# A layer's first residual, computed through DRAM: placed behind the HGRN group, or behind retention's rotation

## The chip, the cores and the metric

The kernel runs on one core of a Trainium2 chip. The metric is the device time of one execution in microseconds (us); lower is better. The kernel before was timed three times: 2478.46 us median, 2472.77 to 2479.16.

## The reference, cut to what matters

Two layers (DEPTH = 2) work on x, 1024 rows by 1024 columns, float32. The part that the change touches is the term `DEEPNORM_ALPHA * h` in the first residual of each layer:

```
h = layer_norm(x, ln_in_g, ln_in_b)
for l in range(DEPTH):
    proj = h @ w_in[l]                       # 13 slices of 256 columns
    y_a = rglru_mixer(a_x, a_g, ...)         # group A, linear scan
    y_b = retention_mixer(r_q, r_k, r_v, r_g, ...)   # group B, rotary on q and k
    y_c = stick_breaking_mixer(s_q, s_k, s_v)        # group C, attention
    y_d = hgrn2_mixer(d_q, d_f, d_v, d_g, ...)       # group D
    mix = jnp.concatenate([y_a, y_b, y_c, y_d], axis=-1) @ w_out[l]
    h = layer_norm(DEEPNORM_ALPHA * h + mix, ln1_g[l], ln1_b[l])
    ff = jnp.square(jax.nn.relu(h @ w_up[l])) @ w_down[l]
    h = layer_norm(DEEPNORM_ALPHA * h + ff, ln2_g[l], ln2_b[l])
```

## The kernel before, in words

Most products run as three float32r matmuls on a high and a low part (`mm3`), so each weight tile is loaded, split by ScalarE (`hi`, L217) and VectorE (`lo`, L218), and multiplied on TensorE.

The normalised rows z of the layer's input are written to a DRAM tile `spill` as they are made (L850 for layer 0, L1285 for layer 1). `residual_spilled` (L815) turns them into `ALPHA * (z * g + b)`: it loads g and b, broadcast, into one 8 KB tile `rgb` (two DMAs, L819), scales it (L820), and then, for each of 16 pieces of 128 by 512, loads a tile `rs` from `spill` (L825), multiplies (L812), adds (L813) and writes it to a second DRAM tile `resid` (L827). All its DMAs are issued from GpSimd's queue (POOL). The output projection reads `resid` much later (L939, SyncE's queue), into the tiles z to which it adds its products (L954).

A layer's trace order is: projection of D's v and g (`proj_d`), `mixer_d`, `residual_spilled`, `mixer_c`, projection of retention's q and k (`proj_b`), `rotary`, projection of its v, projection of A (`proj_a`), `mixer_a`, projection of its g, `mixer_b`, output projection. `mixer_d` works head pair by head pair (hp); for each it makes 6 levels of intra-chunk scores and then a chain of state updates (L492) that feed the matmuls of L501. `mixer_c` goes block by block: scores `ps` (L572, L573), two activations `ca`, `cs` (L577, L578), a scan on VectorE (L580), a transpose (L592) and the product with v (L600).

The order of the instructions on the engines isn't the trace order. The kernel is built with `schedule_with_timeline_sim=True`: a planner simulates the engines and lets each engine take, of what is ready, what comes first in trace order; `boost()` puts a block ahead (the units of D, C, A and B). The order that the planner writes down is then fixed: each engine executes its list in order and waits at the head of it.

Tiles are taken from pools with a fixed number of buffers, and an instruction that opens a tile waits for a free one. Two pools matter here. `m` has 13 buffers of 2 KB: `rs`, D's q, k, f and products, C's `ca` and `cs`, A's `bd`, `axc`, `ar`, `ai`, `aa`. `u` has 4 of 8 KB: D's output `yd`, `rgb`, C's values `cv`, C's output `yc`, the rotation's work tile `rot`, A's output `ya`, B's `yb`. The PSUM pool `po` has one bank, shared by D, C and B.

Of the kernel before, what the change touches and what calls it, by code (L numbers as in the profile page):

```python
# [44 lines left out]
def trunk_kernel(ctx, tc, x, ln_in_g, ln_in_b, w_in, conv_w, conv_b, rg_wa, rg_ba, rg_wx, rg_bx, rg_lambda,  # L45
# [26 lines left out]
    def t_z(shape, nm, dt=F32):  # L72
        return big.tile(shape, dt, tag="z", name=nm, bufs=NZ)

    def t_u(dt, shape, nm):
        return big.tile(shape, dt, tag="u", name=nm, bufs=4)

    def t_m(shape, nm):
        return mid.tile(shape, F32, tag="m", name=nm, bufs=NM)
# [542 lines left out]
    def proj_b(l, act, which, dst):  # L622

        for s in which:
            i = (s - R_Q) % 2
            w = load_cols(w_in[l], seg(s), "wb")
            for pr in range(4):
                ps = gemm_tm_pair(w, act, pr)
                d = dst[pr][:, i]
                if s == R_G:  # L630
                    A.activation(d, ps, AF.Sigmoid)
                    V.tensor_tensor(out=d, in0=ps, in1=d, op=ALU.mult)
                else:
                    A.activation(d, ps, AF.Copy)

    def rotary(qk):

        wk = t_u(F32, [P, 2, 2, 512], "rot")
        for pr in range(4):
            for which in range(2):  # L640
                ct = wk[:, which, 0].rearrange("p (y h d) -> p y h d", y=2, d=32)
                tb = wk[:, which, 1].rearrange("p (h two d) -> p h two d", two=2, d=32)
                nc.sync.dma_start(out=ct, in_=c_rot[pr, which])
                d = qk[pr][:, which].rearrange("p t (h two d) -> p (t h) two d", two=2, d=32)
                V.tensor_tensor(out=tb[:, :, 0, :], in0=d[:, :, 1, :], in1=ct[:, 1], op=ALU.mult)
                V.tensor_tensor(out=tb[:, :, 1, :], in0=d[:, :, 0, :], in1=ct[:, 1], op=ALU.mult)
                V.tensor_tensor(out=d, in0=d, in1=ct[:, 0].unsqueeze(2).to_broadcast([P, 8, 2, 32]), op=ALU.mult)
                V.tensor_tensor(out=d[:, :, 0, :], in0=d[:, :, 0, :], in1=tb[:, :, 0, :], op=ALU.subtract)
                V.tensor_tensor(out=d[:, :, 1, :], in0=d[:, :, 1, :], in1=tb[:, :, 1, :], op=ALU.add)
# [160 lines left out]
    def residual(z, gb, bb):  # L810

        V.tensor_tensor(out=z, in0=z, in1=gb, op=ALU.mult)  # L812
        V.tensor_tensor(out=z, in0=z, in1=bb, op=ALU.add)  # L813

    def residual_spilled(g, b):  # L815

        r = t_u(F32, [P, 2, DM], "rgb")
        for i, v in enumerate((g, b)):
            nc.gpsimd.dma_start(out=r[:, i], in_=v.rearrange("(o d) -> o d", o=1).to_broadcast([P, DM]))  # L819
        V.tensor_scalar(out=r, in0=r, scalar1=ALPHA, scalar2=None, op0=ALU.mult)  # L820
        for nt in range(NT):
            for j in range(2):
                c = slice(512 * j, 512 * j + 512)
                t = t_m([P, 512], "rs")
                nc.gpsimd.dma_start(out=t, in_=spill[nt][:, c])  # L825
                residual(t, r[:, 0, c], r[:, 1, c])
                nc.gpsimd.dma_start(out=resid[nt][:, c], in_=t)  # L827
# [28 lines left out]
    res_g, res_b = ln_in_g, ln_in_b  # L856
# [15 lines left out]
    for l in range(DEPTH):  # L872
# [2 lines left out]
            vt, gt = [], []  # L875
            weave(proj_d(l, act, vt, gt))
        ys[3] = mixer_d(l, act, vt, gt)
        residual_spilled(res_g, res_b)
        ys[2] = mixer_c(l, act)
        qk = [t_z([P, 2, 2, 256], f"bqk{i}") for i in range(4)]  # L880
        proj_b(l, act, (R_Q, R_K), qk)
        rotary(qk)
        vg = [t_z([P, 2, 2, 256], f"bvg{i}") for i in range(4)]
        proj_b(l, act, (R_V,), vg)
        xs, gs = proj_a(l, act)
# [428 lines left out]
        res_g, res_b = ln2_g[l], ln2_b[l]  # L1314
# [66 lines left out]
```

## Time and profile before

| what | value |
|---|---|
| timed runs | 2478.46 us median of 3 |
| profiled execution, its own time | 2481.85 us |
| span of its instructions | 2480.1 us |
| mean granted TensorE clock | 0.982 |
| busy: PE, weight load, VectorE, ScalarE, GpSimd | 96%, 80%, 71%, 45%, 4% |

The span is the time from the first instruction to the last; 1.75 us of the execution lie around it. Durations below come from this one execution. "Granted clock" 1.00 is 2.4 GHz, 0.50 is 1.2 GHz. The rows of layer 0 lie between 100 and 600 us; the same stages of layer 1 come some 1226 us later.

### The profile page before, as it was taken

How to read it: one execution, taken by the hardware profiler on the slowest of the kernel's cores; microseconds unless marked ns; L12 is line 12 of the kernel's file. 1: busy time of each engine (PE TensorE's matmuls, PEld its weight loads, DVE VectorE, ACT ScalarE, POOL GpSimd, SP SyncE). 2: the span in 40 equal slices, each digit the busy share in tenths (PEclk: the TensorE clock that was granted, in tenths of full speed). 3: DMA queues.
4: the chain of work that ended last, by engine and by line, in shares of the span. 5: the costliest groups of instructions: out<-in, count | busy, mean ns of one | idle time of the engine just before them, and what ended most of it. 6: DMA issues, size and time to landing. Idle time of an engine off the chain costs nothing.

```text
span 2480.1 us, 34844 instructions
## 1 busy us (share of the span) xinstructions
PE 2386.4 (96%) x13924; PEld 1980.3 (80%) x13924; DVE 1757.0 (71%) x3016; ACT 1112.4 (45%) x1723; POOL 98.3 (4%) x180
## 2 busy tenths in 40 slices
PE   7999999999899999999999989999998999999997
PEld 6887888877688888888798878888777888888886
DVE  6468773657877877778655788556669777887778
ACT  5433655525543444434462336473264544445342
POOL 0002000000100000000000020000001000000000
PEclk9998999999899999999999989999999999999999
DMA  5215111220742233322212141112217333233322
GB/s 193 57 39 172 47 37 34 86 85 17 256 152 94 77 136 106 132 93 94 94 65 64 57 158 35 29 60 77 68 45 278 132 107 105 92 110 127 111 85 85
DMA packets 126970, 241.30 MB, mean 97 GB/s; under 512 B 8924, under 2 KB 81240, under 8 KB 118616
## 3 DMA queue, kind: packets, MB, share of 16 engines
q1 hardware_dynamic: 106032, 135.55, 17.0%
q0 software_dynamic: 19648, 102.80, 11.5%
q8 instruction: 110, 1.80, 0.3%
q10 hardware_dynamic: 1128, 0.72, 0.1%
q14 instruction: 52, 0.43, 0.1%
HBM read 201.29 MB, written 37.75 MB: 96 GB/s over the span
## 4 chain that ended last, share of the span: by engine, by line
PE 64%; issue 18%; DVE 12%; ACT 3%; DMA 2%; POOL 1%; SPq 0%; DVEq 0%; POOLq 0%; ACTq 0%
PE pg L256 17%; PE pt L256 11%; PE pg L248 8%; PE pg L247 8%; PE pg L249 8%; PE ps L256 5%; DVE z L999 3%; PE po L256 2%; DVE wdl L218 2%; DVE wd L996 1%; DVE u L996 1%; PE po L600 1%; DMA rs<-spill 1%; PE pt L592 1%; PE pt L202 1%
## 5 line engine op out<-in xcount | busy, mean ns | idle before, releaser
L218 DVE TENSOR_TENSOR wul<-wu,wuh 128x1024 fp32r<-128x1024 f32 x106 | 129.6, 1223 | 129.6 <-ACT wuh L217 59.6
L217 ACT ACTIVATE wuh<-wu 128x1024 fp32r<-128x1024 f32 x106 | 112.1, 1059 | 225.6 <-DVE wu L996 138.8
L256 PE MATMUL pg<-wdh,sa 128*128 128x512 f32 x560 | 182.0, 394 | 11.2 <-ACT sa L1189 7.2
L218 DVE TENSOR_TENSOR wdl<-wd,wdh 128x1024 fp32r<-128x1024 f32 x120 | 146.4, 1220 | 44.4 <-PE pt L256 23.2
L217 ACT ACTIVATE wdh<-wd 128x1024 fp32r<-128x1024 f32 x120 | 126.7, 1056 | 106.2 <-PE pg L256 71.6
L256 PE MATMUL ps<-wdh,sa 128*128 128x512 f32 x448 | 148.1, 396 | 8.2 <-ACT sa L1189 7.0
L256 PE MATMUL pt<-wdh,sa 128*128 128x512 f32 x448 | 146.7, 392 | 0.0
L256 PE MATMUL pt<-s,wuh 128*128 128x512 f32 x448 | 137.9, 389 | 0.0
L256 PE MATMUL pg<-s,wuh 128*128 128x512 f32 x448 | 136.1, 389 | 0.0
L256 PEld LDWEIGHTS pg<-wdh,sa 128*128 128x128 f32 x560 | 104.9, 189 | 38.4 <-ACT sa L1189 12.4
L247 PE MATMUL pg<-wo,yh 128*128 128x512 f32 x256 | 104.5, 408 | 9.0 <-DVE z L954 5.2
L256 PE MATMUL pg<-mh,wuh 128*128 128x512 f32 x280 | 108.9, 389 | 0.0
L256 PE MATMUL pg<-ml,wuh 128*128 128x512 f32 x280 | 108.9, 389 | 0.0
L256 PE MATMUL pg<-mh,wul 128*128 128x512 f32 x280 | 108.8, 389 | 0.0
L996 DVE TENSOR_TENSOR sa<-u,sa 128x512 fp32r<-128x512 f32 x140 | 90.9, 686 | 24.7 <-ACT sa L1189 24.7
L256 PEld LDWEIGHTS ps<-wdh,sa 128*128 128x128 f32 x448 | 85.3, 191 | 27.7 <-ACT sa L1189 7.8
L256 PE MATMUL pg<-wdl,sa 128*128 128x512 f32 x280 | 107.4, 392 | 0.0
L248 PE MATMUL pg<-wo,yh 128*128 128x512 f32 x256 | 103.4, 404 | 0.0
L249 PE MATMUL pg<-wo,yl 128*128 128x512 f32 x256 | 101.6, 403 | 0.2 <-DVE yl L899 0.2
L256 PEld LDWEIGHTS pt<-wdh,sa 128*128 128x128 f32 x448 | 85.1, 190 | 17.9
L1189 ACT ACTIVATE sa<-u 128x512 fp32r<-128x512 f32 x140 | 80.1, 623 | 42.4 <-PE pt L256 20.2
L256 PEld LDWEIGHTS pg<-s,wuh 128*128 128x128 f32 x448 | 84.1, 188 | 17.4
(400 smaller groups left out, 6806.2 us busy)
## 6 DMA issues: line engine op xcount, KB each, us to landing
s<-sd POOLq DMA_DIRECT2D x64, 1024.0 KB, 7.4
wu<-in_w_up_dram SPq DMA_DIRECT2D x64, 512.0 KB, 3.7
wd<-in_w_down_dram SPq DMA_DIRECT2D x64, 512.0 KB, 3.6
sd<-sx POOLq DMA_DIRECT2D x32, 512.0 KB, 8.3
spill<-z SPq DMA_DIRECT2D x16, 512.0 KB, 4.4
wb<-in_w_in_dram SPq DMA_DIRECT2D x16, 512.0 KB, 6.5
rs<-spill POOLq DMA_DIRECT2D x32, 256.0 KB, 4.2
resid<-rs POOLq DMA_DIRECT2D x32, 256.0 KB, 3.7
```

What stands on the lines that cost most here:

```text
L202: T.transpose(pt[:, j, i * P:(i + 1) * P], zs[i][:, k * P:(k + 1) * P], ident)
L217: A.activation(hi, raw, AF.Copy)
L218: V.tensor_tensor(out=lo, in0=raw, in1=hi.bitcast(F32), op=ALU.subtract)
L247: T.matmul(ps, ah, bh, start=(i == 0), stop=False)
L248: T.matmul(ps, ah, bl, start=False, stop=False)
L249: T.matmul(ps, al, bh, start=False, stop=(i == n - 1))
L256: T.matmul(ps, a, b, start=(first and i == 0 and j == 0), stop=(i == n - 1 and j == 2), skip_group_check=not first)
L592: T.transpose(pt[:, j * P:(j + 1) * P], s[:, j * P:(j + 1) * P], ident)
L600: T.matmul(po[DH * par:DH * par + DH, (nb % 4) * P:(nb % 4 + 1) * P], vt[:, kb, e:e + DH], wts[par][:, j * P:(j + 1) * P], start=(diag and ...
L996: V.tensor_tensor(out=out, in0=x, in1=y, op=ALU.subtract)
L999: V.tensor_tensor(out=out, in0=x, in1=y, op=ALU.add)
L1189: A.activation(hi, src, AF.Copy)
```

## The change

One call moves down, past `mixer_c`, the projection of retention's q and k, and the rotation. Nothing else is edited; the instructions of `residual_spilled` are the same.

```
         ys[3] = mixer_d(l, act, vt, gt)
-        residual_spilled(res_g, res_b)
         ys[2] = mixer_c(l, act)
         qk = [t_z([P, 2, 2, 256], f"bqk{i}") for i in range(4)]
         proj_b(l, act, (R_Q, R_K), qk)
         rotary(qk)
+        residual_spilled(res_g, res_b)
         vg = [t_z([P, 2, 2, 256], f"bvg{i}") for i in range(4)]
```

With it, the tiles `rgb` and `rs` stand behind `cv`, `yc`, `rot` and all `ca` and `cs` in the order in which the pools are asked.

## Rows read from the trace of the kernel before

**Rows 1.** The page, busy us by engine, with share of the span and count.

```profile
PE 2386.4 (96%) x13924; PEld 1980.3 (80%) x13924; DVE 1757.0 (71%) x3016; ACT 1112.4 (45%) x1723; POOL 98.3 (4%) x180
```

**Rows 2.** Stretches: length; busy us (count) PE, PEld, DVE, ACT, POOL; clock; DMA share; GB/s.

```profile
180.00:224.20 44.20, 44.18 (x573) 37.26 (x571) 39.53 (x89) 14.63 (x30) 14.61 (x27) 1.00 0.58 187
224.20:227.80 3.60, 0.00 (x0) 0.00 (x0) 2.18 (x5) 0.28 (x1) 1.63 (x3) 1.00 0.75 236
227.80:241.40 13.60, 11.35 (x72) 8.74 (x73) 12.65 (x35) 3.93 (x10) 2.17 (x4) 0.50 0.29 108
241.40:364.00 122.60, 121.22 (x1013) 101.81 (x1012) 98.75 (x199) 77.47 (x166) 0.00 (x0) 1.00 0.15 44
364.00:404.00 40.00, 40.00 (x279) 35.21 (x277) 5.56 (x7) 11.83 (x16) 0.00 (x0) 1.00 0.11 31
1449.80:1453.20 3.40, 0.30 (x12) 0.16 (x6) 2.17 (x4) 0.28 (x1) 1.62 (x3) 0.99 0.67 239
1453.20:1466.80 13.60, 10.28 (x69) 7.91 (x70) 13.34 (x36) 3.93 (x10) 2.72 (x5) 0.50 0.35 125
```

**Rows 3.** Chain that ended last, 215 to 242 us: start, us, what.

```profile
220.94 4.52 DMA rs<-spill
...
230.19 3.68 DMA resid<-rs
```

**Rows 4.** Waits, 216 to 241 us: who <- for whom: total us, times, longest.

```profile
ACT ca L577 <- DMA resid<-rs: 6.3, 2, 4.0
...
PE po L501 <- DVE df L492: 4.2, 2, 3.7
...
DVE rs L812 <- DMA rs<-spill: 3.4, 3, 1.5
...
ACT cs L578 <- DMA resid<-rs: 2.6, 1, 2.6
```

**Rows 5.** Waits, 1440 to 1467 us (layer 1).

```profile
ACT ca L577 <- DMA resid<-rs: 4.7, 1, 4.7
```

**Rows 6.** Instructions on tiles rs: count, ns min/median/max, first and last start.

```profile
L825 POOL DMA_DIRECT2D rs<-spill x32: 536/541/555, 183.8 to 1453.3; - x32
L812 DVE TENSOR_TENSOR rs<-rs,rgb x32: 666/685/693, 196.2 to 1458.3; 128x512 f32<-128x512 f32 x32
L813 DVE TENSOR_TENSOR rs<-rs,rgb x32: 676/685/693, 199.9 to 1459.3; 128x512 f32<-128x512 f32 x32
L827 POOL DMA_DIRECT2D resid<-rs x32: 539/544/561, 201.0 to 1460.3; - x32
```

**Rows 7.** The same on tile rgb, and its DMAs from issue to landing.

```profile
L820 DVE TENSOR_SCALAR rgb<-rgb x2: 1226/1226/1227, 194.8 to 1420.3; 128x2048 f32<-128x2048 f32 x2
...
DMA to landing us min/median/max: 6.9/7.6/8.3
```

**Rows 8.** VectorE in order of time, layer 0: start, us, what [idle before <- releaser].

```profile
360.21 0.42 DVE L649 TENSOR_TENSOR bqk<-bqk,rot 128x256 f32<-128x256 f32 x1
...
362.02 0.48 DVE L737 MEMSET bd<- 128x512 f32 x1
...
387.37 1.23 DVE L218 TENSOR_TENSOR wal<-wa,wah 128x1024 fp32r<-128x1024 f32 x1 [23.06 <-ACT wah L217]
```

**Rows 9.** Line 850, the writing of spill in layer 0.

```profile
L850 SPq DMA_DIRECT2D spill<-z x8: 319/360/1042, 12.1 to 34.8; - x8
```

**Rows 10.** Line 600 between 170 and 400 us.

```profile
L600 PE MATMUL po<-ca,cv x288: 272/273/324, 263.8 to 374.1; 128*64 128x128 f32 x144
```

**Rows 11.** Line 939, the reading of resid, both layers.

```profile
L939 SPq DMA_DIRECT2D z<-resid x16: 319/320/339, 462.8 to 1740.6; - x16
```

**Rows 12.** Waits, 290 to 330 us.

```profile
ACT ca L577 <- PE po L600: 9.8, 3, 3.7
...
PE pt L592 <- DVE cs L583: 1.0, 2, 0.6
```

**Rows 13.** ScalarE in order of time, retention's first evacuation.

```profile
258.07 0.60 ACT L634 ACTIVATE bqk<-pg 128x512 f32<-128x512 f32 x1 [3.40 <-DVE dat L509]
```

More of the change, by code (lines that the diff above doesn't have):

```diff
@@ L877, in trunk_kernel @@
         ys[3] = mixer_d(l, act, vt, gt)
-        residual_spilled(res_g, res_b)
         ys[2] = mixer_c(l, act)
@@ L882, in trunk_kernel @@
         rotary(qk)
+        residual_spilled(res_g, res_b)
         vg = [t_z([P, 2, 2, 256], f"bvg{i}") for i in range(4)]
```

## The prediction

> **What bounds the kernel now.** I read the busy line first. TensorE is busy 96% of the span and nothing else is above 71% [rows 1], so time is won only where TensorE stands still, runs at the lower clock, or waits inside a stage. Then I looked for stretches in which it does. Near the end of group D, TensorE does nothing from 224.2 to 227.8, and right behind that its granted clock is 0.50 (1.2 GHz) for 13.6 us; before and after it is busy throughout at 1.00. Layer 1 has the same pair of stretches, 3.4 us with 0.30 busy and 13.6 us at 0.50 [rows 2].
>
> Third, the chain that ended last and the waits say what held it. The chain through these 20 us runs over a load of the residual (4.52 us) and a store of it (3.68 us) [rows 3]. By engine: ScalarE, executing in order, waits 6.3 + 2.6 us to open `ca` and `cs` until stores of `rs` give buffers of pool m back; VectorE waits 3.4 us for loads of `rs`, with D's state updates (L492) queued behind them; TensorE waits 4.2 us for those updates [rows 4]. In layer 1 the `ca` wait is 4.7 us [rows 5]. So the residual does harm in three ways where it stands: 16 tiles through pool m in the middle of the change from D to C, VectorE blocked on DMAs, and VectorE's time itself, in 44 us in which it is 89% busy (39.53 of 44.20) [rows 2].
>
> **The change, part by part.**
>
> *Removed from the old place.* VectorE: 16 x (0.685 + 0.685) + 1.23 = 23.1 us a layer [rows 6, 7]. POOL: 16 x (0.541 + 0.544) = 17.4 us of issue, plus two for `rgb` [rows 6]. What this gives back I take from TensorE alone. Layer 0, 224.2 to 241.4: 17.2 us long; the work done is 0 + 11.35 x 0.50 = 5.7 us of the full clock; lost 11.5 us. Layer 1, 1449.8 to 1466.8: 17.0 us; work 0.3 + 10.28 x 0.50 = 5.4; lost 11.6 us [rows 2]. Together 23.1 us. With the waits gone TensorE should run on at 1.00, and the work behind shifts forward whole, since TensorE is busy 121.22 of the next 122.60 us and 40.00 of the 40 after that [rows 2]. Late next in the old place is D's own chain of state updates, which stays: some of its steps will still come a little late. That part no row prices; it lies between nothing and the 4.2 us that TensorE waits for L492 now [rows 4], and I take 1.0 us a layer, near the low end, because the 3.4 us that VectorE stood blocked on loads were most of it.
>
> *The clock.* It fell after 3.6 us without a matmul and came back 13.6 us later [rows 2], so 6.8 us of each layer's 11.5 are the clock's. The terms hang together: if the idle time goes, so does the low clock.
>
> *Added in the new place, VectorE.* The same 23.1 us. From 364 to 404 VectorE is busy 5.56 of 40 us, with one idle piece of 23.06 us before L218 at 387.37 [rows 2, 8]; room 34.4 us. TensorE is then busy with retention's v and A's projection. What would the cover cost if it were gone: VectorE blocked on an `rs` load at 387 delays the second half of A's weights; the longest such wait now is 1.5 us [rows 4].
>
> *When it can start.* `rgb` needs one of 4 buffers of u. With `yd`, `cv`, `yc` and `rot` ahead of it, the first to come back is `rot` (last use at 360.6) or `cv` (last use 374.1 + 0.3) [rows 8, 10]. So `rgb` is asked at about 361, lands 7.6 us later [rows 7] and is scaled by 370. Pool m has room at that time: `bd`, the first tile behind C's, is opened at 362.02 [rows 8], so loads of `rs` can be issued from then on. 22 us of VectorE from 370 make 392 the earliest end. If it takes as long as now (196.2 to about 234 in layer 0) it ends at 408, 4 us past that stretch. I take about 400 and price it at nothing.
>
> *Queues passed.* On POOL there is nothing between the old and the new place: it is idle from 241 to 404 [rows 2], so its 34 issues stand in nobody's way. On SyncE the first reading of `resid` is at 462.8 [rows 11], some 55 us behind the end that I expect; it would become late only if the residual ran on beyond 460. DMA: the engines are 11% busy there against 58% in the old stretch [rows 2], and the weights of A come through more crowded queues; 0 to 1 us, taken as 0. `rot` no longer waits for `rgb` to be done, worth nothing while TensorE is busy. `ya` takes the other of the two u buffers, free at 374.4, while A's second weights are split only at 387.37 [rows 8]; nothing.
>
> *Sum.* 2481.85 - (23.1 - 2 x 1.0) = 2481.85 - 21.1 = 2460.7 us in the profiled execution's own time. That execution is 3.4 us above the median of the timed runs, so the median should be 2460.7 - 3.4 = 2457.3: **2457 us**, 0.9% less.
>
> [...] I have taken busy matmuls as a full TensorE. The weight loads between 241.4 and 364 are busy 101.81 of 122.60 us, 83% [rows 2]. [...]
>
> **The rivals.**
>
> *A, slower: the loads run ahead of their scale.* Loads of `rs` need only `spill` and a buffer of m. In the old place the first was issued at 183.8, while VectorE first used one at 196.2 [rows 6], so loads do sit and wait for `rgb`. If the planner gives them buffers as soon as D lets go (about 184 to 197) but `rgb` has none until 361, they hold a good part of m's 13 buffers through all of C. For it: the idle POOL takes what is free. Against it: the same loads could have been issued long before 183.8 from `spill`, whose last write is issued at 34.8 [rows 9], and `bd`, which depends on nothing, was opened only behind C's last tiles [rows 8], so the pool seems to serve earlier tiles first. Price: even with 13 buffers C waits three times in 40 us for one (9.8 us on ScalarE), and TensorE then loses 1.0 us, 0.33 a wait [rows 12]. One such wait for each of C's 24 segments makes 8 us a layer; with ScalarE's full 3.25 us each it would be 78. I take 8 and the old stall kept, since its buffers are still missing: 2478.5 + 16 = 2495. It decides from 23.1 / 48 = 0.48 us of TensorE a segment if the old stall goes.
>
> *B, no change: the stall is D's own.* Retention's q and k are first evacuated at 258.07, released by D's last step [rows 13]; TensorE's other work there may be used up whatever the residual does, and D's chain of L492 would leave it idle again, with the low clock behind it. Against: the chain and three of the four waits name the residual's DMAs [rows 3, 4]. The time would be 2478, also if the planner left the residual where it is.
>
> *C, half the gain: a new stall where it lands.* VectorE, blocked on an `rs` load late in its list, holds up A's units; a gap as long as the old one brings the low clock as in [rows 2]. At half the old price, 5.8 us a layer, the median is 2457.3 + 11.6 = 2469. Against: TensorE is busy to the end of that stretch, and nothing that it does there reads what VectorE makes of the residual [rows 2].
>
> **How the numbers follow.** Forecast 0.69, A 0.11, B 0.10, C 0.10. About 0.3% (7.4 us) is what a measurement of this kernel can tell from no change. The forecast and two thirds of C lie below 2471: faster 0.76. B and the rest of C: same 0.13. A: slower 0.11. Range: low end 2457 - 11 = 2446, if D's chain costs nothing (2 us) and another piece of low clock falls away with the new order; the high end takes in C and B, 2479; A is left out.
>
> **What would show it.** Right: TensorE busy and at 1.00 through the end of D in both layers; no wait of `ca` or `cs` for `resid`; L812 first at about 360 (370, less the 11 us by which all behind D comes earlier), last before 400; VectorE's 23 us idle piece filled; z read from `resid` without a wait. Wrong: L825 issued near 185 again (A or B); TensorE waiting for L492 with the clock at 0.50 behind it (B); a new piece at 0.50 between 360 and 440 (C).

## The result, and the profile after

The changed kernel takes **2443.4 us** (median of 4 runs, 2440.3 to 2445.6), against 2475.6 for the kernel before in the same session (median of 4; the forecast went by the first three, 2478.5): ratio 0.9866, 95% interval 0.9846 to 0.9886, so 32 us less. I had forecast 2457 with a range from 2446. The direction and the mechanism of the stall came out, the gain is half as large again, and the time lies below the range. One execution of e3_behind_c, a version below, took 4760.6 us against 2446.6 to 2454.9 for its others, and is left out of its median.

The busy line of the changed kernel, for [rows 1]: TensorE has lost 19 us of busy time on the same 13924 matmuls, so a good part of the gain is clock; VectorE has as much to do as before.

```profile
PE 2367.4 (97%) x13924; PEld 1967.0 (80%) x13924; DVE 1759.4 (72%) x3016; ACT 1115.6 (46%) x1725; POOL 99.4 (4%) x180
```

Three stretches of it, columns as in [rows 2]: the end of D in layer 0, the same in layer 1, and the residual's new place. The pieces with next to no matmul (3.6 and 3.4 us) and the 13.6 us at 0.50 behind each are gone; where the residual now runs, TensorE is busy throughout at 1.00.

```profile
200.00:233.20 33.20, 33.20 (x325) 26.90 (x323) 21.44 (x60) 14.69 (x33) 0.00 (x0) 1.00 0.11 33
1404.00:1438.00 34.00, 34.00 (x330) 27.67 (x330) 22.48 (x63) 14.76 (x32) 0.00 (x0) 1.00 0.11 33
353.20:393.20 40.00, 40.00 (x271) 35.14 (x270) 27.12 (x41) 11.33 (x15) 14.68 (x26) 1.00 0.67 236
```

The residual's instructions, for [rows 6, 7], with the last of layer 0 from VectorE's order of time. The loads are issued at 348.8, behind the two of `rgb`, and the work ends at 384.0, ahead of the 400 that I had allowed.

```profile
L825 POOL DMA_DIRECT2D rs<-spill x32: 536/541/1133, 348.8 to 1572.7; - x32
L812 DVE TENSOR_TENSOR rs<-rs,rgb x32: 621/683/692, 355.0 to 1587.1; 128x512 f32<-128x512 f32 x32
```

```profile
383.35 0.68 DVE L813 TENSOR_TENSOR rs<-rs,rgb 128x512 f32<-128x512 f32 x1
```

**Where the time came from.** I cut each layer at three events: the first matmul of D's intra-chunk scores (L413, their diagonal), A's first activation (L729), and the first row normalised behind the output projection (L962). Windows of the kernel before, then of the changed one, layer 0 and then layer 1. Each pair of stretches holds the same matmuls (2584, then 884), so their lengths can be compared.

```profile
105.55:393.36 287.81, 280.57 (x2584) 236.00 (x2583) 205.50 (x446) 122.80 (x252) 18.41 (x34) 0.98 0.22 67
393.36:564.08 170.72, 162.47 (x884) 134.55 (x883) 98.16 (x260) 76.51 (x99) 0.00 (x0) 0.94 0.22 70
1331.46:1618.45 286.99, 279.86 (x2584) 235.53 (x2583) 205.55 (x446) 122.76 (x253) 18.44 (x34) 0.98 0.21 67
1618.45:1783.05 164.60, 156.82 (x884) 129.94 (x883) 97.63 (x259) 76.42 (x99) 0.00 (x0) 0.98 0.23 72
```

```profile
103.86:380.21 276.35, 275.13 (x2584) 232.24 (x2583) 205.84 (x444) 122.90 (x253) 18.12 (x33) 1.00 0.21 67
380.21:542.36 162.15, 156.64 (x884) 130.60 (x883) 99.09 (x262) 77.86 (x101) 0.81 (x2) 0.98 0.23 78
1308.91:1585.24 276.33, 275.10 (x2584) 232.21 (x2583) 205.74 (x444) 122.91 (x253) 18.17 (x33) 1.00 0.21 67
1585.24:1747.57 162.33, 156.64 (x884) 130.62 (x883) 98.81 (x261) 77.86 (x101) 0.82 (x2) 0.98 0.24 78
```

The first stretch (D and C) gives 11.5 + 10.7 = 22.1 us (before rounding): that is nearly the gain I forecast (21.1). The second (A, retention, output projection), on which I had put nothing, gives 8.6 and 2.3 us more. That was the surprise that the experiments had to settle.

### The profile page after: what moved, and what is told of

Its sections match the earlier page's. It is cut to its first block, busy times and chain, and to the rows that moved or that the text cites. A ratio compares the mean times of both kernels' runs of the same rounds, so it can differ in the third digit from the quotient of the medians.

```text
span 2443.8 us, 34888 instructions
## 1 busy us (share of the span) xinstructions
PE 2367.4 (97%) x13924; PEld 1967.0 (80%) x13924; DVE 1759.4 (72%) x3016; ACT 1115.6 (46%) x1725; POOL 99.4 (4%) x180
## 3 DMA queue, kind: packets, MB, share of 16 engines
q0 software_dynamic: 19648, 102.80, 11.5%
## 4 chain that ended last, share of the span: by engine, by line
PE 62%; issue 21%; DVE 13%; ACT 1%; DMA 1%; POOL 1%; DVEq 0%; SPq 0%; POOLq 0%; ACTq 0%
PE pg L256 17%; PE pt L256 10%; PE pg L248 7%; PE pg L247 7%; PE pg L249 7%; PE ps L256 5%; DVE z L999 3%; PE po L256 2%; DVE wdl L218 2%; PE po L600 2%; PE pt L592 1%; DVE wd L996 1%; DVE u L996 1%; PE ps L407 1%; DVE sa L996 1%
## 5 line engine op out<-in xcount | busy, mean ns | idle before, releaser
L256 PEld LDWEIGHTS pg<-wdh,sa 128*128 128x128 f32 x560 | 105.5, 190 | 40.8 <-ACT sa L1189 12.4
L256 PEld LDWEIGHTS pt<-s,wuh 128*128 128x128 f32 x448 | 84.1, 188 | 17.4
```

The source lines that it names most:

```text
L256: T.matmul(ps, a, b, start=(first and i == 0 and j == 0), stop=(i == n - 1 and j == 2), skip_group_check=not first)
```

## The experiments

Times are medians; ratios are to the kernel before in the same session, with 95% intervals. "D and C" and "later stage" are the two stretches above in the profiled execution, layer 0 / layer 1. "Order" is the planner's list of TensorE's instructions from retention's first scores to the first normalised rows: "old" is the list of the kernel before, "new" that of the changed one, line for line; other lists are called "own".

| kernel | us | ratio | D and C | later stage | order |
|---|---|---|---|---|---|
| before, profile shown | 2475.6 | 1 | 287.8 / 287.0 | 170.7 / 164.6 | old |
| e8_copy | 2474.8 | 0.9995 [0.9985, 1.0005] | 288.0 / 287.0 | 164.5 / 164.4 | old |
| changed kernel | 2443.4 | 0.9866 [0.9846, 0.9886] | 276.4 / 276.3 | 162.2 / 162.3 | new |
| e1_none | 2454.3 | 0.9906 [0.9889, 0.9922] | 276.4 / 276.4 | 164.4 / 166.2 | old |
| e2_layer0 | 2464.6 | 0.9948 [0.9934, 0.9963] | 276.3 / 287.0 | 162.2 / 167.8 | new / old |
| d1_double | 2463.1 | 0.9949 [0.9935, 0.9962] | 287.8 / 286.9 | 159.1 / 159.0 | new |
| v1_new_no_dve | 2455.8 | 0.9916 [0.9903, 0.9928] | 276.3 / 276.3 | 166.6 / 164.7 | old |
| e5_old_no_dve | 2460.4 | 0.9935 [0.9923, 0.9947] | 278.8 / 283.7 | 166.7 / 166.6 | old |
| e10_old_dve_only | 2461.3 | 0.9935 [0.9923, 0.9948] | 280.8 / 281.4 | 165.8 / 162.3 | old |
| e4_own_z12 | 2504.6 | 1.0112 [1.0096, 1.0128] | 299.0 / 297.9 | 165.5 / 168.1 | own |
| e6_behind_v | 2444.4 | 0.9869 [0.9854, 0.9883] | 276.4 / 276.3 | 159.1 / 164.0 | new |
| e7_behind_a | 2443.7 | 0.9867 [0.9849, 0.9885] | 276.3 / 276.3 | 161.0 / 160.8 | new |
| e3_behind_c | 2451.9 | 0.9899 [0.9881, 0.9917] | 276.5 / 276.8 | 162.2 / 163.5 | own |
| p2_new_pool | 2486.1 | 1.0037 [1.0024, 1.0051] | 276.3 / 276.4 | 183.4 / 185.6 | own |

**The kernel before once more, and no residual at all.** e8_copy adds only a comment. e1_none takes the call out:

```
-        residual_spilled(res_g, res_b)
...
-            nc.sync.dma_start(out=z, in_=resid[nt])
+            nc.sync.dma_start(out=z, in_=spill[nt])
```

> The kernel before, unchanged, for a second profile. Same time within 3 us. Layer 0 from A's last ya to the first zu: 101 us again if its two pieces of low clock (10.2 and 10.2 us) belong to the order of its instructions, about 95 as in layer 1 if they were chance of that execution.

> The residual is left out altogether: z is read from spill, unscaled, so its time is a floor for every place of the residual. Theory (the residual is hidden whole behind retention's rotation): within 4 us of the changed kernel, about 2440; D's end 11.5 us a layer earlier than before. Rival (it still costs where it now stands, since A's last ya came 2.3 us a layer late): 2432 to 2437. The surplus over the forecast, if it is the planner's new order of group B and the output projection once the residual is gone from the old place, shows here too: from A's last ya to the first zu 91 us in both layers (before: 101.4 and 95.3). If it was chance of one execution: 95 or more in some layer.

The copy stands at 1 and puts the chance into numbers: with the same list, its later stage of layer 0 is 6.2 us shorter than in the profile that I had read. e1_none was the lesson: it leaves out 23 us a layer of VectorE's work and all of the residual's loads and stores, has the same D and C as the changed kernel, and is still 10 to 11 us slower. Both of its forecasts missed, since I had expected it equal or faster. So the changed kernel has a gain that removing the residual doesn't give.

**The new place in layer 0 alone.**

```
+        if l == 1:
+            residual_spilled(res_g, res_b)
         ys[2] = mixer_c(l, act)
...
+        if l == 0:
+            residual_spilled(res_g, res_b)
```

> New place in layer 0 alone, old place in layer 1. Theory: each layer has its own gain. Layer 0 as in the changed kernel (D's end -11.5, from A's last ya to the first zu 91 us), layer 1 as before (stall of 17 us at the end of D with the clock at 0.50, then 95 us). Time 2475.6 - 11.5 - (5 to 8) = 2456 to 2459. Rival (the surplus is chance, not tied to the place): 2464, and the 91 us stretch does not go with the layer.

Each layer behaves by its own place: 276.3 and 287.0 us for D and C. The list of layer 0's later stage is the new one (162.2), that of layer 1 the old one (167.8). The time missed the theory's 2456 to 2459: 2464.6 is the rival's number, though the rival's sign (a later stage that does not go with the layer) did not come. Layer 0's stall and the mean saving of the new list (4.7 us, below) would make 16 us; the gain is 12 (interval 9 to 16), and the 167.8 us of layer 1 are among the longest that the old list shows.

**Taking the two gains apart.** d1_double leaves the residual where it was and adds a second one in the new place, whose result nothing reads (to the kernel before); v1_new_no_dve takes the multiplications and additions out of the changed kernel.

```
+    resid2 = dpool.tile([NT, P, DM], F32, name="resid2")
...
         rotary(qk)
+        residual_spilled(res_g, res_b, resid2)
```

```
-                residual(t, r[:, 0, c], r[:, 1, c])
```

> The residual stands in the old place, as before, and a second one of the same size stands in the new place and writes to a tensor that nothing reads (so this kernel does more work than either). The order that the planner writes for the retention and output-projection stage is then that of the changed kernel, while the old place keeps its stall. Theory (two separate gains: the stall at D's end, 11.5 us a layer, and the planner's other order of the stage from A's last result to the first normalised row, 95 to 101 us with the old order and 90.6 with the new, against 2.2 us more in A): D's second head pair ends 65 us behind its first as before, the later stage takes 90.5 us, and the time is some 8 us below the kernel before (about 2467, ratio 0.997). Rival (the later stage got shorter because the stall went, or by chance pieces of low clock): that stage takes 95 us or more, time 2475 or above. Rival two (23 us of VectorE in the new place do cost something): above 2478.

> The residual in the new place with its loads, stores and the scaling of the two vectors, but without the 32 multiplications and additions (left out, so the rows are added unscaled). The planner then writes the old order for the retention and output-projection stage. Theory (two separate gains): the stall at D's end is gone (53.6 us from the first head pair's end to the second's), the later stage takes 95 to 97 us as before, and the time is about 2454, that of the kernel without any residual, some 10 us ABOVE the changed kernel although it does 22 us a layer less on VectorE. Rival (the gain of the later stage belongs to the place and not to the order): 90.6 us in that stage and a time of 2443 or less.

Their windows of layer 0, d1_double first; columns as above.

```profile
105.47:393.23 287.76, 280.72 (x2584) 235.94 (x2583) 225.35 (x477) 122.79 (x253) 36.60 (x67) 0.98 0.30 97
393.23:552.36 159.13, 153.61 (x884) 127.91 (x883) 99.10 (x262) 77.74 (x101) 0.82 (x2) 1.00 0.24 80
```

```profile
105.23:381.57 276.34, 275.11 (x2584) 232.20 (x2583) 187.48 (x414) 122.88 (x253) 18.95 (x34) 1.00 0.22 69
381.57:548.12 166.55, 158.54 (x884) 131.34 (x883) 98.35 (x260) 76.55 (x99) 0.00 (x0) 0.97 0.22 72
```

They cross as the theory of two gains says. The double residual keeps the whole old stall and has later stages as short as any here (159.1 and 159.0 us): it does 46 us a layer of VectorE work where the kernel before does 23, and is 13 us faster (I had expected 8). The light one loses the stall and has the old list and the old later stage: 12 us slower than the changed kernel with 22 us a layer less to do. So the second gain belongs to the planner's list, and it is VectorE's work in the new place that changes the list: with loads and stores alone there (v1_new_no_dve) it stays the old one. It is not TensorE's list alone: ScalarE's order in the later stage is one and the same wherever the table says "old", and another wherever it says "new". By which of its steps the planner comes to the new list, no run shows.

What the new list saves is seen in TensorE's waits of layer 0, of e8_copy and then of the changed kernel (from 440 to 562 us; who <- for whom: total, times, longest):

```profile
PE ps L671 <- ACT bqT L664: 2.6, 2, 1.8
PE pg L247 <- DVE z L954: 2.1, 2, 1.5
PE pg L247 <- ACT yh L898: 1.9, 1, 1.9
...
PE po L677 <- DVE bsc L672: 0.2, 1, 0.2
```

```profile
PE ps L671 <- ACT bqT L664: 1.7, 2, 1.5
PE po L677 <- DVE bsc L672: 1.6, 1, 1.6
PE pg L247 <- DVE z L954: 1.2, 1, 1.2
...
PE pg L247 <- ACT yh L898: 0.2, 1, 0.2
```

Between retention's last core and its last transposes (L710) the old list holds 56 matmuls of the output projection, the new one 74; the wait for `yh`, the split of retention's last output, falls from 1.9 to 0.2 us. The waits for `bqT` and z fall by 0.9 us each, and the one for `bsc` grows by 1.4. Over all profiles here the later stage takes 165.8 us with the old list (13 stretches, 162.3 to 170.7) and 161.1 with the new one (9 stretches, 159.0 to 164.0). TensorE's idle time in it (length less busy) is 7.3 against 5.6 us; the other 3.0 us of the 4.7 are busy time at a lower clock. What in the list keeps the clock up, no run shows.

**What makes the stall in the old place.** e5_old_no_dve keeps loads, stores and buffers and leaves out VectorE's work; e10_old_dve_only keeps VectorE's work, on one tile, and leaves out loads and stores; e4_own_z12 does all of it, with `rs` in a pool of its own of 2 buffers (and one buffer of z less, for room).

```
-                residual(t, r[:, 0, c], r[:, 1, c])
```

```
+        t = t_m([P, 512], "rs")
+        V.memset(t, 0.0)
...
-                t = t_m([P, 512], "rs")
-                nc.gpsimd.dma_start(out=t, in_=spill[nt][:, c])
...
-                nc.gpsimd.dma_start(out=resid[nt][:, c], in_=t)
...
-            nc.sync.dma_start(out=z, in_=resid[nt])
+            nc.sync.dma_start(out=z, in_=spill[nt])
```

```
-                t = t_m([P, 512], "rs")
+                t = rpool.tile([P, 512], F32, tag="rs", name="rs", bufs=2)
```

> The residual in the old place with its loads, its stores and its 16 buffers of m, but without the 32 multiplications and additions (left out). It tells which of the three harms makes the stall. If VectorE does it (its 22 us of work, and standing blocked on loads with D's state updates behind it): the second head pair ends 54 us behind the first, and the time is about 2454. If the buffers of m do it (ca and cs waiting for stores): 63 us or more, the waits of ca and cs for stores of rs stay at 4 us or more, and the time is 2470 or more. If each does half: about 59 us and 2463.

> In the old place only VectorE's part of the residual: the two vectors are loaded and scaled, and the 32 multiplications and additions run on one tile, with no load, no store and 15 buffers of m less (the residual itself is left out; z is read unscaled). The planner's order of the later stage is that of the kernel before. From the first head pair's end to A's first activation the kernel before takes 200.5 us (199.6 in layer 1), the changed one 189.0, and the old place with loads, stores and buffers but without VectorE's work 191.5 and 196.4. Theory (two harms that each make part of the stall, and together bring the low clock): 193 to 197 us, time 2459 to 2466. Rival one (VectorE's own 22 us are the whole stall, since D's state updates stand behind them): 199 or more, 2472 or more. Rival two (only DMAs hurt, as loads that VectorE stands blocked on and as buffers held until stores are done): 189 to 190 us, 2454 or less.

> Old place, but rs has two buffers of its own (one buffer fewer in the pool of z), so it takes none of pool m. Theory 'buffers of m' : no wait of ca or cs for resid, TensorE busy through the end of D, 15 to 23 us gained in the two layers (2453 to 2461). Rival 'VectorE': L812 still waits for loads and L492 stands behind them, TensorE idle 3 us or more and the clock at 0.50 behind it, gain under 8 us.

TensorE's waits at D's end, layer 0. The kernel before has two, 4.2 us for L492 [rows 4] and one for `cs`:

```profile
PE ps L572 <- ACT cs L578: 1.6, 1, 1.6
```

e5_old_no_dve has the second alone; with it ScalarE's wait to open `cs` there, and a wait of TensorE in layer 1 (1400 to 1480 us) for which the profile names no releaser:

```profile
PE ps L572 <- ACT cs L578: 2.1, 1, 2.1
```

```profile
ACT cs L578 <- DMA resid<-rs: 3.2, 2, 2.8
```

```profile
PE ps L407 <- issue: 1.7, 1, 1.7
```

Then e10_old_dve_only, and e4_own_z12, whose lines are numbered two higher (its L503 is L501 of the kernel before, its L494 is L492):

```profile
PE po L501 <- DVE df L492: 1.7, 3, 1.0
PE pg L247 <- DVE cq L550: 1.2, 1, 1.2
```

```profile
PE po L501 <- DVE dat L510: 9.3, 1, 9.3
PE po L503 <- DVE df L494: 4.3, 3, 2.7
```

```profile
DVE rs L814 <- DMA rs<-spill: 15.1, 10, 3.4
```

Each harm alone costs less than both together: D and C are 2.4 and 7.3 us (layer 0, layer 1) above the undisturbed 276.35 with loads, stores and buffers alone, 4.4 and 5.1 with VectorE's work alone, 11.5 and 10.7 with both. They don't add up to the whole, 6.9 against 11.5 us in layer 0 and 12.4 against 10.7 in layer 1, and the 7.3 us hold the wait of 1.7 us at L407 and a piece of low clock behind it, whose cause no run shows. So both harms are shown, their shares are not. Taken alone each shows its own wait: `cs`, which waits for stores of `rs`, or the state updates L492. My numbers for e10_old_dve_only named a badly chosen stretch: its 189.4 and 190.1 us are about rival two's, but it began at the first head pair's end, which itself came 4 us later there while TensorE was busy throughout; its time, 2461.3, is the one expected by two harms. e4_own_z12 missed both of its forecasts, being slower than the kernel before. The private pool took the waits of `ca` and `cs` for stores away and made the other harm worse: with only two loads of `rs` under way VectorE stands blocked on loads for 15.1 us (last line above, from 190 to 262 us; 4.0 in the kernel before) with D's units queued behind it. What the missing buffer of z adds is not taken apart.

**Other places.** The same call behind the projection of retention's v, behind A's projection, and right behind C:

```
         proj_b(l, act, (R_V,), vg)
+        residual_spilled(res_g, res_b)
```

```
         xs, gs = proj_a(l, act)
+        residual_spilled(res_g, res_b)
```

```
         ys[2] = mixer_c(l, act)
+        residual_spilled(res_g, res_b)
```

> The residual one step further down, behind the projection of retention's v. The planner's order of the retention and output-projection stage is that of the changed kernel. Theory: both gains stay (53.6 us at D's end, 90.6 us in the later stage), and the time is that of the changed kernel, 2443, give or take 4. Rival (the new place matters, since the residual's VectorE work now starts later and runs into A's stage): A's stage, 71.6 us from its first activation to its last result in layer 1, gets 3 us or more longer, and the time is 2450 or more.

> The residual behind A's projection, so that its 23 us of VectorE run inside A's mixer. The planner's order of matmuls in the later stage is that of the changed kernel. Theory (VectorE's work is hidden as long as TensorE has other products to do): 53.6 us at D's end, 159 to 164 us from A's first activation to the first normalised row, time 2443 give or take 4. Rival (VectorE, now with A's units and the splits of w_out beside the residual, becomes late): TensorE is idle more than 7 us in that stretch (5.3 to 5.8 us in the changed kernel), and the time is 2450 or more.

> The residual right behind the stick-breaking group (C), before the projection of retention's q and k. The planner writes a third order for the retention and output-projection stage, which ends, like the changed kernel's, with 74 products of the output projection in one piece behind retention's last core. Theory (stall at D's end gone once the residual is out of the old place, 53.6 us from the first head pair's end to the second's; the rest decided by the order of the later stage): from A's first activation to the first normalised row 159 to 164 us, like the kernels with 74 products at the end, and a time of 2440 to 2447. Rival (the distance from D counts: so close behind C, the loads of rs still hold buffers of m that C or A needs): the first head pair's end to A's first activation is longer than 189.0 us, and the time is 2450 or more.

The two later places equal the changed kernel. Right behind C it is 8 us slower. Buffers of m are hardly the reason (D and C take 276.5 and 276.8 us). VectorE's residual work now stands where TensorE waits for the rotation, a wait that the changed kernel does not have, and its own list waits longer for `bsc` (e3_behind_c, 365 to 560 us):

```profile
PE po L677 <- DVE bsc L672: 2.6, 1, 2.6
...
PE pt L662 <- DVE bqk L649: 1.2, 1, 1.2
```

In all, TensorE stands idle some 2 us a layer longer than in the changed kernel: 7.3 and 7.0 us against 5.5 and 5.7 in the later stage, and 0.3 and 0.6 us more in D and C, where shorter waits of C's transposes (L592) make up for most of the one for the rotation. The profiled execution was the fastest of this kernel (2446.6 us); what the others, up to 2454.9, lose beyond it stays open. Both theories missed here: the time was the rival's, but its reason was not seen.

**The residual's arithmetic on GpSimd, in the new place.**

```
-                residual(t, r[:, 0, c], r[:, 1, c])
+                nc.gpsimd.tensor_tensor(out=t, in0=t, in1=r[:, 0, c], op=ALU.mult)
+                nc.gpsimd.tensor_tensor(out=t, in0=t, in1=r[:, 1, c], op=ALU.add)
```

> The residual in the new place with its 32 multiplications and additions on GpSimd, so that VectorE has none of them and GpSimd alone runs the whole residual. Nothing is left out. Theory: VectorE's part of the residual was hidden in the new place, so taking it from VectorE gives nothing by itself; the stall at D's end stays gone (53.6 us); the planner's order of the later stage is a third one, with the 56 products at the end of the old order, so that the wait for yh (1.9 us) is back: 164 to 167 us from A's first activation to the first normalised row, against 162 in the changed kernel, time 2449 to 2456. Rival (VectorE free in A's stage is worth something): 159 us or less and a time of 2440 or less. Third (GpSimd is so slow that z is read late): output-projection idle on z by more than 5 us, time over 2465.

All three expectations missed: 2486, slower than the kernel before. The third's time (over 2465) came, but not its reason: TensorE waited only 1.0 us for z in that stage. VectorE's own instructions grew while GpSimd computed. VectorE's split of A's weights between 360 and 402 us, in p2_new_pool and in the changed kernel (ns min/median/max), and GpSimd's instructions from 355 to 410 us (busy us, mean ns):

```profile
L218 DVE TENSOR_TENSOR wal<-wa,wah x2: 2311/4572/6832, 374.3 to 381.0; 128x1024 fp32r<-128x1024 f32 x2
```

```profile
L218 DVE TENSOR_TENSOR wal<-wa,wah x2: 1224/1224/1225, 374.2 to 375.7; 128x1024 fp32r<-128x1024 f32 x2
```

```profile
L827 POOL TENSOR_TENSOR rs<-rs,rgb 128x512 f32<-128x512 f32 x16 | 22.3, 1404 | 0.1
L826 POOL TENSOR_TENSOR rs<-rs,rgb 128x512 f32<-128x512 f32 x16 | 20.4, 1292 | 0.2
```

A's first unit begins at 400.2 us, against 380.8 in the changed kernel (L755). The slow splits are one part of that. The other is an order of its own: VectorE's list here holds the split of the second weights ahead of the units, and VectorE sits idle 11.3 us before it, behind ScalarE's half of that split:

```profile
394.69 5.01 DVE L218 TENSOR_TENSOR wbl<-wb,wbh 128x1024 fp32r<-128x1024 f32 x2 [11.34 <-ACT wbh L217]
399.76 0.48 DVE L737 MEMSET bd<- 128x512 f32 x1
400.17 0.98 DVE L755 TENSOR_SCALAR axc<-axa,pcol 128x512 f32<-128x512 f32 x1
```

TensorE then waits where it did not before, or longer (436 to 500 us), with the clock at 0.90 over the whole later stage:

```profile
PE pt L710 <- DVE bym L706: 3.7, 1, 3.7
PE po L677 <- DVE bsc L672: 3.5, 1, 3.5
PE ps L763 <- DVE axc L760: 2.6, 2, 2.0
```

TensorE's own list differs too: from retention's first scores to the first normalised rows it has 454 instructions, against 588 in the old list, as fewer products of other stages stand between retention's cores. How much of the loss is GpSimd's and how much the list's, no run shows.

None of these versions beats the changed kernel: the best two equal it within 1 us.

## Why the prediction was wrong

- **The stall at D's end: right, and its size nearly so.** Forecast 23.1 less 2 x 1.0 = 21.1 us; measured 22.1 on the profiles shown. Two small errors stand against each other in it: layer 1 gave 10.7 us where 11.6 were counted, and the discount for D's own chain was not needed. In the six kernels whose residual is behind the rotation or left out, D and C take 276.3 to 276.4 us in both layers, and in the changed one no wait for L492 is left. e5_old_no_dve and e10_old_dve_only bear out that buffers and VectorE's work both do harm, as the prediction had it.
- **The clock: right in kind.** The pieces of 13.6 us at 0.50 went with the gaps ahead of them. The share given to the clock, 6.8 us of a layer's 11.5, is too large: TensorE was busy 11.35 and 10.28 us of those 13.6, so the low clock cost 5.7 and 5.1 us and the rest was idle time. The sum does not use that share.
- **The cost in the new place: right at nothing** for the stretch that I named: with C behind D it takes the same 276.35 us as without any residual. `rgb` was asked at 347.8 (forecast 361 less 11 = 350), the first multiplication came at 355.0 (forecast about 360). The margin before `resid` is read was reckoned from 408 us (55 us), not from the 400 that I expected (63).
- **"The work behind shifts forward whole": this step failed.** It holds up to A's first activation. Behind it the planner wrote another list, and that stage got shorter by 4.7 us a layer, 9.5 in all (with an uncertainty of about 1.6 a layer, from the spread of the 13 and 9 stretches). The sum then is 22.1 + 9.5 = 31.6, against 32.2 measured. In my sum a new order stood at nothing; only the low end of the range let another piece of low clock go with it, without a row to price it (11 us, D's discount included). The measured time lies 2.6 us below that end.
- **The profile against the median.** The 36.3 us between the two profiled spans (2480.1 and 2443.8) hold about 5 us of chance: the later stage of layer 0 took 170.7 us in the profile before, 164.5 in its copy and 165.8 on the mean of the old list. Another 3.3 us lie outside the stretches: 1.7 ahead of D's first scores, and 0.8 in each layer behind the first normalised rows; I did not follow them. The base moved as well: off the 2475.6 us of all four executions the same sum gives 2454.5, which misses too.
- **Full or not.** The prediction noted that the weight loads were busy 83% of the stretch behind the stall. That held little of the gain back: D and C shortened by 11.5 and 10.7 us, where TensorE had lost 11.5 and 11.6.
- **The rivals.** A (loads ahead of their scale) did not happen: the planner issued `rgb` and then the loads. B and C neither: no stall of D's own, no new gap in the new place.

## What to carry to other kernels

When a planner writes the order, moving a block changes two things: the stalls where it stood, which the trace prices well, and the list of everything behind it, which the trace does not show. Compare the lists, or, as here, run the kernel without the block and the kernel with the block doubled, before a gain is put down to the work that was moved. And leaving work out is no floor: e1_none and v1_new_no_dve do less and are slower.

## What the runs showed of the hardware

**The same list of matmuls loses a different amount to the clock each time.** The later stage of e6_behind_v, layer 0 and then layer 1, one execution, the same order: 153.6 us busy at 1.00, and 158.2 at 0.97.

```profile
380.20:539.28 159.08, 153.63 (x884) 127.92 (x883) 99.08 (x262) 77.74 (x101) 0.82 (x2) 1.00 0.24 79
1580.37:1744.32 163.95, 158.16 (x884) 131.86 (x883) 99.03 (x261) 77.85 (x100) 0.82 (x2) 0.97 0.23 77
```

So single stretches of one profile carry some 5 us of chance, and a list that saves 1.7 us of idle time may be worth 3.0 us of clock beside it (the means above). The Trainium skill (TensorE: Matmul & The Clock Gate, "The HAM clock gate") calls the cold stretch at a kernel's start variable from run to run; here it holds in the middle of a kernel, and between two layers of one run.

**VectorE instructions with two SBUF inputs wait while GpSimd computes.** The two splits took 2.31 and 6.83 us in place of 1.22, while GpSimd's own took 1.29 and 1.40 on the mean. The Trainium skill (SBUF — State Buffer, "SBUF: two separate sides") says that the two engines share a port pair as an exclusive lock, held for a whole instruction. The trace agrees that VectorE is held up, and shows more than one GpSimd instruction's worth of it.
